# The product-key top-k of an expert layer, with its candidate sums, index arithmetic and lookup made for four heads in one set of instructions

## The chip, the cores and the metric

One core of a Trainium2 chip. The time is device microseconds (us) for one execution of the whole program; lower is better. Of each kernel there is a median of several runs, and one further execution that the hardware profiler recorded.

## What is computed

A decoder trunk of two layers over 256 tokens of width 1024. Each layer has a mixer half (a state-space mixer and two attentions) and an expert half. The expert half is where the change lies. For each token and each of 8 heads it scores two sets of 128 keys, takes the 16 best of either, adds the two lists to candidates, takes the 16 best sums, and looks up which pair of keys each one came from:

```python
q = (xc @ wq).reshape(PEER_CHUNK, PEER_HEADS, 2, PEER_HALF)
s1 = einsum("thd,nd->thn", q[:, :, 0], k1)
s2 = einsum("thd,nd->thn", q[:, :, 1], k2)
v1, i1 = top_k(s1, 16)
v2, i2 = top_k(s2, 16)
cand = (v1[..., :, None] + v2[..., None, :]).reshape(..., 256)
sc, ci = top_k(cand, 16)
e = take_along_axis(i1, ci // 16) * 128 + take_along_axis(i2, ci % 16)
g = softmax(sc)
act = gelu(einsum("td,thkd->thk", xc, u[e])) * g
out = einsum("thk,thkd->td", act, v[e])
```

The kernel gathers nothing: it computes the products with all 16,384 rows of `u` and `v` and weighs them with a matrix of gates built from `e` and `g`.

## The kernel before

Tokens lie on the 128 partitions in two chunks (`NC`), or in the free dimension where channels are on the partitions. Every fp32 product is made of three matmuls (`mm3`, lines 165 to 168): a weight tile is fetched, ScalarE rounds it to a high part (`split`, L159, tile `wH`), VectorE or GpSimd subtracts to get the low part (L162, tile `wL`), and TensorE runs high times high, low times high, high times low. `wH` and `wL` have three buffers each.

The expert half of a layer (`peer`) goes through these steps on TensorE, in the order in which the code is written (a manual schedule for that engine alone; the other engines' queues are ordered by the framework's scheduler):

1. The queries of head 0, then for each head the queries of the next head and the scores of this one (`query`, `scores`). A query is 48 matmuls over two weight tiles. The low part of these tiles is made on GpSimd in two halves of 512 columns.
2. With the last head the first pair of rows of `u` (`u_pair(0)`), then the pairs 1 to 17. A pair is 48 matmuls over two weight tiles of 1024 columns, with the low parts made on GpSimd (`low="gg"`), and a Gelu on ScalarE (L695).
3. Transposes of the found indices `fi` and of the softmax weights `scv` (L794, L795), which ScalarE casts to `idx1`, `idx2`, `wh` (L796 to L798).
4. Pairs 18 and 19, and then the gates, step by step with the other 44 pairs; after them the products with `v`.

On VectorE the top-k runs beside steps 1 and 2. `choose(h, sc)` is called once for each head. `top16` finds 16 maxima and their places with five instructions (`MAX8`, `FIND_INDEX8`, `MATCH_REPLACE8`, `MAX8`, `FIND_INDEX8`), four times per head on 128 scores (tile `sc`) and twice per head on 80 candidates (`cand`). Beside these, each call has 14 other instructions:

- three sums that make the candidates (L742 to L744, 32, 112 and 16 elements per partition),
- a cast of the found places to 16 bits (L750, `fii`, 64 elements),
- seven small steps of index arithmetic on 32 elements (L752 to L761: tiles `r8`, `a0`, `hi`, `fab`; the profile prints a tile's name without digits at its end),
- the lookup: a comparison with a ramp (L764, `eq`, 1024 elements of 16 bits), a product (L765) and a sum (L766, into `fi`).

After the last head come a subtraction of the maximum (L781), the exponential on ScalarE (L783, placed behind the Gelu of pair 15 by `issue_after(gelu[-3])`), and the division (L785 to L788). ScalarE's queue is in order: what stands behind L783 there is the next casts of `wH`.

Of the kernel before, what the change touches and what calls it, by code (L numbers as in the profile page):

```python
# [12 lines left out]
F16 = mybir.dt.float16  # L13
F32 = mybir.dt.float32
F32R = mybir.dt.float32r
U32 = mybir.dt.uint32
AF = mybir.ActivationFunctionType
ALU = mybir.AluOpType
AX = mybir.AxisListType
# [3 lines left out]
P = 128  # L23
D = 1024
S = 256
NC = 2
# [4 lines left out]
PH = 8  # L31
TK = 16
# [5 lines left out]
AHEAD = 3  # L38
GI = 2
NCAND = 80  # L40
RB = 5
RATE = 2.0
PT = (0, 0)
# [39 lines left out]
def trunk(ctx: ExitStack, tc: tile.TileContext, x_in, c_in, ada, cols, rows, w_in, w_out, wq, keysT, uT, vT, fg, out, dbg=None):  # L83
    nc = tc.nc
    V, A, G, T = nc.vector, nc.scalar, nc.gpsimd, nc.tensor
# [25 lines left out]
    iotar = const.tile([P, TK, TK], F16, tag="iotar", name="iotar")  # L111
# [561 lines left out]
    def peer(l, steps):  # L673
# [23 lines left out]
        with tc.tile_pool(name=f"topk{l}", bufs=1, reuse_waits="tile") as tp:  # L697
            def new(shape, tag, dt=F32, bufs=1):
                return tp.tile(shape, dt, tag=tag, name=tag, bufs=bufs)
# [6 lines left out]
            def top16(vals, idx, src):  # L706
                V.max(vals[:, 0:8], src)
                V.max_index(idx[:, 0:8], vals[:, 0:8], src)
                V.match_replace(out=src, in_to_replace=vals[:, 0:8], in_values=src, imm_value=-3.0e38)
                V.max(vals[:, 8:16], src)  # L710
                V.max_index(idx[:, 8:16], vals[:, 8:16], src)
# [3 lines left out]
            def query(h):  # L715
                with pinned() if h == 0 else nullcontext():
                    pq = proj_channels(wq[l], h * D * 256, 256, lambda q: "h")
                q = new([P, 2, S], "q", bufs=2)
                for i in range(2):
                    A.copy(q[:, i, :], pq[i][:, :S])  # L720
                return q
# [7 lines left out]
                A.copy(sc, pscr.rearrange("p (a b) -> p a b", a=4))  # L729
                return sc  # L730

            def choose(h, sc):
                vv = new([P, 2, NC, TK], "vv", bufs=2)
                ii = new([P, 2, NC, TK], "ii", U32, bufs=2)
                for c in range(NC):
                    for i in range(2):
                        top16(vv[:, i, c, :], ii[:, i, c, :], sc[:, 2 * c + i, :])


                cand = new([P, NC, NCAND], "cand", bufs=2)  # L740
                v1, v2 = vv[:, 0], vv[:, 1]
                V.tensor_tensor(out=cand[:, :, 0:16], in0=v1[:, :, 0:1].to_broadcast([P, NC, TK]), in1=v2, op=ALU.add)  # L742
                V.tensor_tensor(out=cand[:, :, 16:72].rearrange("p c (a b) -> p c a b", b=8), in0=v1[:, :, 1:8, None].to_broadcast([P, NC, 7, 8]), in1=v2[:, :, None, 0:8].to_broadcast([P, NC, 7, 8]), op=ALU.add)
                V.tensor_tensor(out=cand[:, :, 72:80], in0=v1[:, :, 8:16], in1=v2[:, :, 0:1].to_broadcast([P, NC, 8]), op=ALU.add)  # L744
                ci = new([P, NC, TK], "ci", U32, bufs=2)
                for c in range(NC):
                    top16(scv[:, c, h, :], ci[:, c, :], cand[:, c, :])

                fii = new([P, 2, NC, TK], "fii", F16, bufs=2)
                V.tensor_copy(fii, ii)  # L750
                r8 = new([P, NC, TK], "r8", U32, bufs=2)
                V.tensor_single_scalar(r8, ci, 3, op=ALU.logical_shift_right)  # L752
                a0 = new([P, NC, TK], "a0", bufs=2)
                V.tensor_scalar(out=a0, in0=r8, scalar1=-1.0, scalar2=0.0, op0=ALU.add, op1=ALU.max)
                hi = new([P, NC, TK], "hi", bufs=2)
                V.tensor_scalar(out=hi, in0=ci, scalar1=-72.0, scalar2=0.0, op0=ALU.add, op1=ALU.max)
                fab = new([P, 2, NC, TK], "fab", F16, bufs=2)
                V.tensor_tensor(out=fab[:, 0], in0=a0, in1=hi, op=ALU.add)
                V.scalar_tensor_tensor(out=a0, in0=a0, scalar=1.0, in1=a0, op0=ALU.min, op1=ALU.add)
                V.scalar_tensor_tensor(out=a0, in0=a0, scalar=-8.0, in1=ci, op0=ALU.mult, op1=ALU.add)  # L760
                V.tensor_tensor(out=fab[:, 1], in0=a0, in1=hi, op=ALU.subtract)  # L761
                eq = new([P, 2 * NC, TK, TK], "eq", F16, bufs=2)
                wide = lambda x: x.rearrange("p i c s -> p (i c) s")
                V.tensor_tensor(out=eq, in0=wide(fab)[:, :, :, None].to_broadcast([P, 2 * NC, TK, TK]), in1=iotar[:, None].to_broadcast([P, 2 * NC, TK, TK]), op=ALU.is_equal)  # L764
                V.tensor_tensor(out=eq, in0=eq, in1=wide(fii)[:, :, None, :].to_broadcast([P, 2 * NC, TK, TK]), op=ALU.mult)  # L765
                V.tensor_reduce(out=wide(fi[:, :, :, h, :]), in_=eq, axis=AX.X, op=ALU.add)  # L766

            q = query(0)
            for h in range(PH):
                q2 = query(h + 1) if h + 1 < PH else None  # L770
                if q2 is None:
                    u_pair(0, act1[:, 0:2, :])
                choose(h, scores(q))
                q = q2
            gelu = [u_pair(ip, act1[:, 2 * ip:2 * ip + 2, :]) for ip in range(1, NA // 2 - LEAD)]


# [262 lines left out]
```

## Time and profile before

| what | us |
|---|---|
| median of 3 runs (lowest, highest) | 1995.51 (1990.01, 1998.99) |
| profiled execution, its own time | 1995.14 |
| its span from first to last instruction | 1993.4 |
| mean granted TensorE clock, of full speed | 0.973 |
| top-k of layer 0, first maximum to last division on VectorE | 198.5 to 353.1 |
| top-k of layer 1, the same | 1184.4 to 1340.2 |

Times of an event count from the span's start. A busy engine is one with an instruction in flight: TensorE's matmuls are pipelined, so that one lasts 284 ns in the list of groups while they start 118 ns apart at full clock and 214 ns apart at half clock. An instruction that waits for a shared resource after it was issued counts as busy, so a wait of that kind shows as a long duration and not as idle time.

### The profile page before, as it was taken

What the parts mean: (1) busy time and instruction counts of PE and PEld (TensorE: products, weight loads), DVE (VectorE), ACT (ScalarE), POOL (GpSimd) and SP (SyncE); (2) the same over time, 40 slices, a digit from 0 to 9 for tenths busy, and PEclk for the clock granted to TensorE, in tenths of its full rate; (3) what the DMA queues carried; (4) which work ended last, traced back from release to release, by engine and by line L of the source; (5) the groups of instructions that cost most, each with busy time, mean ns of one, the idle gap of its engine ahead of it and who ended that gap; (6) DMA issues with size and microseconds to landing.
All of it is one profiled execution on the core that took longest, in us unless ns stands there. A gap on an engine that the chain in (4) does not pass through costs nothing.

```text
span 1993.4 us, 33885 instructions
## 1 busy us (share of the span) xinstructions
PE 1883.4 (94%) x12864; PEld 1717.4 (86%) x12864; DVE 1440.0 (72%) x2746; ACT 966.0 (48%) x1502; POOL 776.0 (39%) x441
## 2 busy tenths in 40 slices
PE   4898998999999998999989989989999999999998
PEld 3787998999999786788877889979999998888886
DVE  6975999889963998855554669998899435555555
ACT  3564544454444444454545544445444444555444
POOL 5775787000024234322246657960000342222333
PEclk9898999999999999999989989989999999999999
DMA  8863554444455998855634334544444555665653
GB/s 285 281 208 124 164 181 165 134 162 155 160 168 177 348 350 311 295 196 193 194 121 138 127 130 149 189 150 155 155 160 159 177 181 190 206 215 192 195 194 116
DMA packets 103559, 376.50 MB, mean 189 GB/s; under 512 B 12002, under 2 KB 12258, under 8 KB 102756
## 3 DMA queue, kind: packets, MB, share of 16 engines
q1 hardware_dynamic: 103396, 374.34, 55.7%
q8 instruction: 100, 1.64, 0.3%
q14 instruction: 63, 0.52, 0.1%
HBM read 371.15 MB, written 3.15 MB: 188 GB/s over the span
## 4 chain that ended last, share of the span: by engine, by line
PE 69%; DVE 21%; POOL 3%; issue 2%; ACT 2%; DMA 2%; SPq 0%; POOLq 0%; ACTq 0%; DVEq 0%
PE pacc L167 11%; PE pacc L168 10%; PE pacc L166 10%; PE pu L166 9%; PE pu L168 9%; PE pu L167 9%; POOL wL L162 2%; PE pa L167 1%; DVE eq L765 1%; PE pa L168 1%; PE pa L166 1%; DVE eq L764 1%; DVE raw L178 1%; DVE fi L766 1%; DVE a L760 1%
## 5 line engine op out<-in xcount | busy, mean ns | idle before, releaser
L162 POOL TENSOR_TENSOR wL<-raw,wH 128x1024 fp32r<-128x1024 f32 (+2 forms) x364 | 719.8, 1992 | 1142.9 <-ACT wH L159 1134.3
L159 ACT CAST wH<-raw 128x1024 fp32r<-128x1024 f32 (+1 forms) x602 | 628.5, 1045 | 517.7 <-PE pu L167 345.2
L166 PE MATMUL pu<-hH,wH 128*128 128x256 f32 x2048 | 581.5, 284 | 4.8 <-ACT wH L159 2.8
L168 PE MATMUL pu<-hH,wL 128*128 128x256 f32 x2048 | 576.2, 281 | 3.8 <-POOL wL L162 3.8
L167 PE MATMUL pu<-hL,wH 128*128 128x256 f32 x2048 | 575.0, 281 | 0.0
L162 DVE TENSOR_TENSOR wL<-raw,wH 128x1024 fp32r<-128x1024 f32 x324 | 399.3, 1233 | 130.9 <-ACT wH L159 130.8
L167 PE MATMUL pacc<-wL,aH 128*128 128x512 f32 x1024 | 401.4, 392 | 11.6 <-POOL wL L162 8.7
L168 PE MATMUL pacc<-wH,aL 128*128 128x512 f32 x1024 | 399.3, 390 | 0.0
L166 PEld LDWEIGHTS pu<-hH,wH 128*128 128x128 f32 x2048 | 387.5, 189 | 5.3 <-ACT wH L159 3.0
L168 PEld LDWEIGHTS pu<-hH,wL 128*128 128x128 f32 x2048 | 388.0, 189 | 4.3 <-POOL wL L162 4.3
L167 PEld LDWEIGHTS pu<-hL,wH 128*128 128x128 f32 x2048 | 388.1, 189 | 0.0
L880 DVE TENSOR_TENSOR aL<-act,aH 128x256 fp32r<-128x256 f32 x256 | 164.1, 642 | 224.2 <-ACT aH L879 223.7
L166 PE MATMUL pacc<-wH,aH 128*128 128x512 f32 x1024 | 277.7, 389 | 1.2 <-ACT wH L159 1.2
L879 ACT CAST aH<-act 128x256 fp32r<-128x256 f32 x256 | 103.9, 407 | 357.0 <-PE pacc L167 354.7
L167 PEld LDWEIGHTS pacc<-wL,aH 128*128 128x128 f32 x1024 | 192.8, 188 | 57.4 <-POOL wL L162 11.7
L166 PEld LDWEIGHTS pacc<-wH,aH 128*128 128x128 f32 x1024 | 191.9, 188 | 41.4 <-ACT wH L159 1.6
L168 PEld LDWEIGHTS pacc<-wH,aL 128*128 128x128 f32 x1024 | 192.8, 188 | 39.6
L166 PE MATMUL pa<-hH,wH 128*128 128x256 f32 x256 | 75.4, 308 | 13.8 <-ACT hH L260 10.9
L167 PE MATMUL pa<-hL,wH 128*128 128x256 f32 x256 | 76.8, 303 | 1.8 <-DVE hL L261 1.8
L168 PE MATMUL pa<-hH,wL 128*128 128x256 f32 x256 | 76.3, 301 | 1.5 <-POOL wL L162 1.5
L178 DVE SCALAR_TENSOR_TENSOR adaw<-adaw,crow 128x1024 f32<-128x1024 f32 x56 | 70.0, 1259 | 1.2 <-ACT crow L130 1.2
L841 DVE SCALAR_TENSOR_TENSOR act<-pc,act 128x160 f32<-128x160 f32 (+30 forms) x126 | 38.4, 305 | 41.2 <-PE pc L835 40.7
(428 smaller groups left out, 2498.6 us busy)
## 6 DMA issues: line engine op xcount, KB each, us to landing
raw<-in_uT_dram SPq DMA_DIRECT2D x256, 512.0 KB, 3.5
raw<-in_vT_dram SPq DMA_DIRECT2D x256, 512.0 KB, 4.2
adaw<-in_ada_dram SPq DMA_DIRECT2D x56, 512.0 KB, 6.1
raw<-in_ada_dram SPq DMA_DIRECT2D x40, 512.0 KB, 4.5
raw<-in_w_in_dram SPq DMA_DIRECT2D x38, 512.0 KB, 4.1
raw<-in_wq_dram SPq DMA_DIRECT2D x32, 512.0 KB, 3.5
raw<-in_w_out_dram SPq DMA_DIRECT2D x16, 512.0 KB, 3.5
raw<-in_w_in_dram SPq DMA_DIRECT2D x8, 392.0 KB, 3.9
```

Of the source, the lines that this page charges most:

```text
L159: A.copy(h[:, :n], src)
L162: eng.tensor_tensor(out=lo[:, o:o + step], in0=src[:, o:o + step], in1=h[:, o:o + step].bitcast(F32), op=ALU.subtract)
L166: T.matmul(o, l[0], r[0], start=start, stop=False)
L167: T.matmul(o, l[0], r[1], start=False, stop=False)
L168: T.matmul(o, l[1], r[0], start=False, stop=stop)
L178: V.scalar_tensor_tensor(out=src, in0=src, scalar=1.0, in1=cond, op0=ALU.mult, op1=ALU.mult, accum_out=modc[:, m, k:k + 1])
L760: V.scalar_tensor_tensor(out=a0, in0=a0, scalar=-8.0, in1=ci, op0=ALU.mult, op1=ALU.add)
L764: V.tensor_tensor(out=eq, in0=wide(fab)[:, :, :, None].to_broadcast([P, 2 * NC, TK, TK]), in1=iotar[:, None].to_broadcast([P, 2 * NC, TK, ...
L765: V.tensor_tensor(out=eq, in0=eq, in1=wide(fii)[:, :, None, :].to_broadcast([P, 2 * NC, TK, TK]), op=ALU.mult)
L841: V.scalar_tensor_tensor(out=a, in0=pv[:, lo:hi, :], scalar=1.0 / WSCALE, in1=a, op0=ALU.mult, op1=ALU.mult)
L879: A.copy(aH, act)
L880: V.tensor_tensor(out=aL, in0=act, in1=aH.bitcast(F32), op=ALU.subtract)
```

## The change

`choose` is called for a group of `GH` = 4 heads instead of one. It first takes the maxima of the four heads, head by head, as their scores come (`next_scores` issues the next head's queries and this head's scores in the same order as before). Then the 14 other instructions are issued once for the whole group, on tiles four times as long, with the candidates' `top16` still once for each head and chunk between them. The tiles of this part have one buffer where they had two.

```diff
+GH = 4
...
-            def choose(h, sc):
-                vv = new([P, 2, NC, TK], "vv", bufs=2)
-                ii = new([P, 2, NC, TK], "ii", U32, bufs=2)
+            def choose(g, scs):
+                hs4 = slice(g * GH, (g + 1) * GH)
+                vv = new([P, 2, NC, GH, TK], "vv")
+                ii = new([P, 2, NC, GH, TK], "ii", U32)
+                for j, sc in enumerate(scs):
+                    sc = sc()
+                    for c in range(NC):
+                        for i in range(2):
+                            top16(vv[:, i, c, j, :], ii[:, i, c, j, :], sc[:, 2 * c + i, :])
+                CG = NC * GH
+                flat = lambda x: x.rearrange("p c h s -> p (c h) s")
+                cand = new([P, CG, NCAND], "cand")
+                v1, v2 = flat(vv[:, 0]), flat(vv[:, 1])
+                V.tensor_tensor(out=cand[:, :, 0:16], in0=v1[:, :, 0:1].to_broadcast([P, CG, TK]), in1=v2, op=ALU.add)
+                V.tensor_tensor(out=cand[:, :, 16:72].rearrange("p c (a b) -> p c a b", b=8), in0=v1[:, :, 1:8, None].to_broadcast([P, CG, 7, 8]), in1=v2[:, :, None, 0:8].to_broadcast([P, CG, 7, 8]), op=ALU.add)
+                V.tensor_tensor(out=cand[:, :, 72:80], in0=v1[:, :, 8:16], in1=v2[:, :, 0:1].to_broadcast([P, CG, 8]), op=ALU.add)
...
-                    top16(scv[:, c, h, :], ci[:, c, :], cand[:, c, :])
+                    for j in range(GH):
+                        top16(scv[:, c, g * GH + j, :], ci[:, c, j, :], cand[:, c * GH + j, :])
...
-                eq = new([P, 2 * NC, TK, TK], "eq", F16, bufs=2)
+                eq = new([P, 2 * CG, TK, TK], "eq", F16)
+                full = [P, 2 * CG, TK, TK]
+                V.tensor_tensor(out=eq, in0=fab.rearrange("p i c s -> p (i c) s")[:, :, :, None].to_broadcast(full), in1=iotar[:, None].to_broadcast(full), op=ALU.is_equal)
+                V.tensor_tensor(out=eq, in0=eq, in1=fii.rearrange("p i c h s -> p (i c h) s")[:, :, None, :].to_broadcast(full), op=ALU.mult)
+                V.tensor_reduce(out=fi[:, :, :, hs4, :].rearrange("p i c h s -> p (i c) (h s)"), in_=eq.rearrange("p (q h) s a -> p q (h s) a", h=GH), axis=AX.X, op=ALU.add)
-            q = query(0)
-            for h in range(PH):
-                q2 = query(h + 1) if h + 1 < PH else None
-                if q2 is None:
-                    u_pair(0, act1[:, 0:2, :])
-                choose(h, scores(q))
-                q = q2
+            qs = [query(0)]
+            def next_scores(h):
+                if h + 1 < PH:
+                    qs.append(query(h + 1))
+                else:
+                    u_pair(0, act1[:, 0:2, :])
+                return scores(qs[h])
+            for g in range(PH // GH):
+                choose(g, [lambda h=h: next_scores(h) for h in range(g * GH, (g + 1) * GH)])
```

The order of instructions on TensorE, ScalarE, GpSimd and SyncE is the same in both programs; only VectorE's differs, and there only within the top-k of the two layers. Three places of layer 0 follow. In the changed program the lines of the sums are L749 to L751, of the cast L759, of the arithmetic L761 to L770, of the lookup L773 to L775, and every line before `choose` is one higher (L707 is L708).

VectorE, behind the maxima of the first scores: before, the rest of head 0 begins right behind its own maxima.

```order
L707 MAX vv<-sc 128x8 x4
L708 MAX_INDEX ii<-vv,sc 128x8 x4
L743 TENSOR_TENSOR cand<-vv 128x2x56
L709 MATCH_REPLACE sc<-vv,sc 128x128 x4
L710 MAX vv<-sc 128x8 x4
L711 MAX_INDEX ii<-vv,sc 128x8 x3
L744 TENSOR_TENSOR cand<-vv 128x2x8
L711 MAX_INDEX ii<-vv,sc 128x8
L742 TENSOR_TENSOR cand<-vv 128x2x16
L750 CAST fii<-ii 128x64
```

Of the change, the same engine where the first sum stands (the maxima of three heads, 60 instructions, lie ahead of these rows):

```order
L708 MAX vv<-sc 128x8 x4
L709 MAX_INDEX ii<-vv,sc 128x8 x4
L750 TENSOR_TENSOR cand<-vv 128x8x56
L710 MATCH_REPLACE sc<-vv,sc 128x128 x4
L711 MAX vv<-sc 128x8 x4
L712 MAX_INDEX ii<-vv,sc 128x8 x3
L751 TENSOR_TENSOR cand<-vv 128x8x8
L712 MAX_INDEX ii<-vv,sc 128x8
L749 TENSOR_TENSOR cand<-vv 128x8x16
L759 CAST fii<-ii 128x256
```

The sums moved from behind the first head to the fourth, and each covers eight rows of 80 candidates instead of two.

VectorE, the first lookup, before (of head 0) and then of the change (of heads 0 to 3):

```order
L764 TENSOR_TENSOR eq<-fab,iotar 128x1024
L708 MAX_INDEX ci<-scv,cand 128x8 x2
L707 MAX vv<-sc 128x8 x4
L765 TENSOR_TENSOR eq<-eq,fii 128x1024
L709 MATCH_REPLACE cand<-scv,cand 128x80 x2
L708 MAX_INDEX ii<-vv,sc 128x8 x4
L743 TENSOR_TENSOR cand<-vv 128x2x56
L766 TENSOR_REDUCE fi<-eq 128x4x16
```

```order
L773 TENSOR_TENSOR eq<-fab,iotar 128x4096
L712 MAX_INDEX ii<-vv,sc 128x8 x4
L708 MAX vv<-sc 128x8 x4
L774 TENSOR_TENSOR eq<-eq,fii 128x4096
L709 MAX_INDEX ii<-vv,sc 128x8 x4
L750 TENSOR_TENSOR cand<-vv 128x8x56
L775 TENSOR_REDUCE fi<-eq 128x4x64
```

The comparison and the product now work on 4096 elements each; maxima of the last heads stand between them.

VectorE, the end of the top-k, before and then of the change:

```order
L761 TENSOR_TENSOR fab<-a_2702,hi 128x32
L758 TENSOR_TENSOR fab<-a_2825,hi 128x32
L764 TENSOR_TENSOR eq<-fab,iotar 128x1024
L759 SCALAR_TENSOR_TENSOR a_2825<-a_2825 128x32
L765 TENSOR_TENSOR eq<-eq,fii 128x1024
L760 SCALAR_TENSOR_TENSOR a_2825<-a_2825,ci 128x32
L766 TENSOR_REDUCE fi<-eq 128x4x16
L761 TENSOR_TENSOR fab<-a_2825,hi 128x32
L764 TENSOR_TENSOR eq<-fab,iotar 128x1024
L765 TENSOR_TENSOR eq<-eq,fii 128x1024
L766 TENSOR_REDUCE fi<-eq 128x4x16
L785 TENSOR_REDUCE zs<-scv 128x16
```

```order
L795 TENSOR_TENSOR scv<-scv,mxs 128x128
L763 TENSOR_SCALAR a_2681<-r_2679 128x128
L767 TENSOR_TENSOR fab<-a_2681,hi 128x128
L768 SCALAR_TENSOR_TENSOR a_2681<-a_2681 128x128
L769 SCALAR_TENSOR_TENSOR a_2681<-a_2681,ci 128x128
L770 TENSOR_TENSOR fab<-a_2681,hi 128x128
L773 TENSOR_TENSOR eq<-fab,iotar 128x4096
L774 TENSOR_TENSOR eq<-eq,fii 128x4096
L775 TENSOR_REDUCE fi<-eq 128x4x64
L799 TENSOR_REDUCE zs<-scv 128x16
```

Before, the last two heads' arithmetic and lookups are woven into each other; now one set of instructions for four heads stands there, with no maxima between the comparison and the product.

## Rows read from the trace of the kernel before

**Rows 1.** The page: busy time of each engine, and the shares of the chain of work that ended last, by engine.

```profile
PE 1883.4 (94%) x12864; PEld 1717.4 (86%) x12864; DVE 1440.0 (72%) x2746; ACT 966.0 (48%) x1502; POOL 776.0 (39%) x441
...
PE 69%; DVE 21%; POOL 3%; issue 2%; ACT 2%; DMA 2%; SPq 0%; POOLq 0%; ACTq 0%; DVEq 0%
```

**Rows 2.** Busy time by stretch, around the top-k of layer 0 and then of layer 1. Columns: from:to, length, busy us and instructions of PE, PEld, DVE, ACT and POOL, granted TensorE clock, DMA share, GB/s.

```profile
240.00:330.00 90.00, 90.00 (x767) 90.00 (x766) 90.00 (x263) 43.30 (x51) 79.33 (x32) 1.00 0.55 182
...
341.00:354.40 13.40, 6.89 (x30) 6.22 (x31) 12.14 (x11) 3.88 (x6) 8.37 (x4) 0.50 0.46 157
...
1229.00:1236.00 7.00, 4.92 (x29) 4.74 (x28) 7.00 (x32) 2.80 (x5) 2.35 (x1) 0.76 0.45 150
...
1331.00:1341.20 10.20, 2.31 (x12) 1.73 (x12) 8.98 (x10) 1.80 (x3) 4.95 (x3) 0.66 0.50 171
```

**Rows 3.** TensorE in order of time, layer 0 and then layer 1: the first transpose of step 3, the first matmul of pair 18, and the first matmul at full clock behind it. Columns: start, duration, engine, line, operation, tiles, shape, count, and the idle time before it with what ended it.

```profile
352.23 0.69 PE L794 MATMUL pc<-ident,fi 128*128 128x128 f32 x2 [5.36 <-DVE fi L766]
...
354.00 0.56 PE L166 MATMUL pu<-hH,wH 128*128 128x256 f32 x1
...
358.16 0.28 PE L167 MATMUL pu<-hL,wH 128*128 128x256 f32 x1
...
1339.16 0.66 PE L794 MATMUL pb<-ident,fi 128*128 128x128 f32 x2 [7.71 <-DVE fi L766]
...
1340.77 0.56 PE L166 MATMUL pu<-hH,wH 128*128 128x256 f32 x1
...
1344.67 0.28 PE L166 MATMUL pu<-hH,wH 128*128 128x256 f32 x1
```

**Rows 4.** ScalarE in order of time, the same columns: the cast that TensorE's end of pair 15 released, and the exponential; layer 0, then layer 1.

```profile
328.10 1.05 ACT L159 CAST wH<-raw 128x1024 fp32r<-128x1024 f32 x1 [1.78 <-PE pu L167]
...
337.98 0.42 ACT L783 ACTIVATE scv<-scv 128x256 f32<-128x256 f32 x1 [7.03 <-DVE scv L781]
...
1317.83 1.05 ACT L159 CAST wH<-raw 128x1024 fp32r<-128x1024 f32 x1 [1.77 <-PE pu L167]
...
1324.77 0.42 ACT L783 ACTIVATE scv<-scv 128x256 f32<-128x256 f32 x1 [4.09 <-DVE scv L781]
```

**Rows 5.** VectorE's groups by line and shape from 197 to 353 us, the 13 of the 14 instructions per head whose durations vary. Columns: line, engine, operation, tiles, shape, count, busy us, mean ns of one, idle us before them.

```profile
L765 DVE TENSOR_TENSOR eq<-eq,fii 128x1024 f16<-128x1024 f16 x8 | 13.3, 1657 | 0.0
L764 DVE TENSOR_TENSOR eq<-fab,iotar 128x1024 f16<-128x1024 f16 x8 | 10.7, 1335 | 0.0
...
L760 DVE SCALAR_TENSOR_TENSOR a<-a,ci 128x32 f32<-128x32 f32 x8 | 9.3, 1168 | 0.0
L742 DVE TENSOR_TENSOR cand<-vv 128x32 f32<-128x32 f32 x8 | 9.2, 1152 | 0.0
...
L750 DVE CAST fii<-ii 128x64 f16<-128x64 uint32 x8 | 8.4, 1046 | 0.0
L744 DVE TENSOR_TENSOR cand<-vv 128x16 f32<-128x16 f32 x8 | 8.3, 1034 | 0.0
L754 DVE TENSOR_SCALAR a<-r 128x32 f32<-128x32 uint32 x8 | 7.9, 992 | 0.0
L743 DVE TENSOR_TENSOR cand<-vv 128x112 f32<-128x112 f32 x8 | 7.4, 924 | 0.0
...
L758 DVE TENSOR_TENSOR fab<-a,hi 128x32 f16<-128x32 f32 x8 | 6.3, 791 | 0.0
L752 DVE TENSOR_SCALAR r<-ci 128x32 uint32<-128x32 uint32 x8 | 6.1, 768 | 0.0
L759 DVE SCALAR_TENSOR_TENSOR a<-a 128x32 f32<-128x32 f32 x8 | 5.1, 632 | 0.0
L761 DVE TENSOR_TENSOR fab<-a,hi 128x32 f16<-128x32 f32 x8 | 4.7, 583 | 0.0
...
L756 DVE TENSOR_SCALAR hi<-ci 128x32 f32<-128x32 uint32 x8 | 2.5, 310 | 0.0
```

**Rows 6.** Single lines over both layers: count, shortest/median/longest duration in ns, first and last start.

```profile
L744 DVE TENSOR_TENSOR cand<-vv x16: 148/1060/1899, 203.1 to 1303.9; 128x16 f32<-128x16 f32 x16
...
L764 DVE TENSOR_TENSOR eq<-fab,iotar x16: 1202/1213/3295, 217.5 to 1333.7; 128x1024 f16<-128x1024 f16 x16
L765 DVE TENSOR_TENSOR eq<-eq,fii x16: 667/686/2872, 219.8 to 1337.1; 128x1024 f16<-128x1024 f16 x16
```

**Rows 7.** In order of time, columns as in rows 3: GpSimd and VectorE where a comparison begins with a low part, GpSimd's usual pace, and VectorE behind the comparison that ended at 296.1.

```profile
278.35 3.48 POOL L162 TENSOR_TENSOR wL<-raw,wH 128x1024 fp32r<-128x1024 f32 x1 [0.42 <-ACT wH L159]
...
278.35 1.21 DVE L764 TENSOR_TENSOR eq<-fab,iotar 128x1024 f16<-128x1024 f16 x1
...
312.27 2.42 POOL L162 TENSOR_TENSOR wL<-raw,wH 128x1024 fp32r<-128x1024 f32 x1 [0.42 <-ACT wH L159]
...
296.06 2.48 DVE L743 TENSOR_TENSOR cand<-vv 128x112 f32<-128x112 f32 x1
```

**Rows 8.** ScalarE in order of time, two casts two tiles apart.

```profile
305.48 1.05 ACT L159 CAST wH<-raw 128x1024 fp32r<-128x1024 f32 x1 [1.78 <-PE pu L167]
...
311.13 1.05 ACT L159 CAST wH<-raw 128x1024 fp32r<-128x1024 f32 x1 [1.78 <-PE pu L167]
```

**Rows 9.** A stall of TensorE in the products with `v` of layer 0 (columns as in rows 3), and the stretch around it (columns as in rows 2).

```profile
692.15 0.50 PE L167 MATMUL pacc<-wL,aH 128*128 128x512 f32 x1 [1.63 <-DVE wL L162]
...
686.00:696.00 10.00, 8.37 (x37) 6.60 (x37) 10.00 (x15) 4.08 (x6) 2.53 (x1) 1.00 0.88 298
```

More of the change, by code (lines that the diff above doesn't have):

```diff
@@ L730, in scores @@
                 return sc
-            def choose(h, sc):
-                vv = new([P, 2, NC, TK], "vv", bufs=2)
-                ii = new([P, 2, NC, TK], "ii", U32, bufs=2)
-                for c in range(NC):
[L736 to L746, printed above, removed]
-                    top16(scv[:, c, h, :], ci[:, c, :], cand[:, c, :])
-                fii = new([P, 2, NC, TK], "fii", F16, bufs=2)
+            def choose(g, scs):
[14 more added lines that the diff above has]
+                V.tensor_tensor(out=cand[:, :, 72:80], in0=v1[:, :, 8:16], in1=v2[:, :, 0:1].to_broadcast([P, CG, 8]), op=ALU.add)
+                ci = new([P, NC, GH, TK], "ci", U32)
+                for c in range(NC):
+                    for j in range(GH):
+                        top16(scv[:, c, g * GH + j, :], ci[:, c, j, :], cand[:, c * GH + j, :])
+                ci = flat(ci)
+                fii = new([P, 2, NC, GH, TK], "fii", F16)
@@ L750, in choose @@
                 V.tensor_copy(fii, ii)
-                r8 = new([P, NC, TK], "r8", U32, bufs=2)
+                r8 = new([P, CG, TK], "r8", U32)
                 V.tensor_single_scalar(r8, ci, 3, op=ALU.logical_shift_right)
-                a0 = new([P, NC, TK], "a0", bufs=2)
+                a0 = new([P, CG, TK], "a0")
                 V.tensor_scalar(out=a0, in0=r8, scalar1=-1.0, scalar2=0.0, op0=ALU.add, op1=ALU.max)
-                hi = new([P, NC, TK], "hi", bufs=2)
+                hi = new([P, CG, TK], "hi")
@@ L756, in choose @@
                 V.tensor_scalar(out=hi, in0=ci, scalar1=-72.0, scalar2=0.0, op0=ALU.add, op1=ALU.max)
-                fab = new([P, 2, NC, TK], "fab", F16, bufs=2)
+                fab = new([P, 2, CG, TK], "fab", F16)
                 V.tensor_tensor(out=fab[:, 0], in0=a0, in1=hi, op=ALU.add)
@@ L761, in choose @@
                 V.tensor_tensor(out=fab[:, 1], in0=a0, in1=hi, op=ALU.subtract)
-                eq = new([P, 2 * NC, TK, TK], "eq", F16, bufs=2)
[L763 to L766, printed above, removed]
-            q = query(0)
-            for h in range(PH):
-                q2 = query(h + 1) if h + 1 < PH else None
-                if q2 is None:
+                eq = new([P, 2 * CG, TK, TK], "eq", F16)
[8 more added lines that the diff above has]
+                else:
                     u_pair(0, act1[:, 0:2, :])
-                choose(h, scores(q))
-                q = q2
+                return scores(qs[h])
+            for g in range(PH // GH):
+                choose(g, [lambda h=h: next_scores(h) for h in range(g * GH, (g + 1) * GH)])
             gelu = [u_pair(ip, act1[:, 2 * ip:2 * ip + 2, :]) for ip in range(1, NA // 2 - LEAD)]
```

## Prediction

> **What bounds the kernel now.** I read the page first. TensorE is busy 94% of the span, but 21% of the chain that ended last lies on VectorE [rows 1], so there are stretches in which TensorE is not what sets the end. The stretches around the top-k show where. From 240 to 330 us TensorE and VectorE are both busy all the time, at full clock, and GpSimd for 79 of 90 us; from 341 to 354.4 TensorE is busy for half the time and has half its clock; layer 1 shows the same from 1331 to 1341.2 [rows 2]. The timeline names what it waits for: the transposes of the found indices stood 5.36 us in layer 0 and 7.71 us in layer 1 until VectorE had made `fi` [rows 3], and before that the exponential stood 7.03 and 4.09 us in ScalarE's queue until VectorE had made its input, with the casts for TensorE's next tiles behind it [rows 4]. So each top-k ends on VectorE.
>
> Next, why VectorE takes 155 us for it. The 13 instructions of a head whose durations vary add up to 99.2 us for the 8 heads [rows 5]. Their shortest durations are far below their means: 148 ns against 1034 for the sum of 16 elements, 1202 for the comparison, 667 against 1657 for the product [rows 5, 6]. With about 0.17 us for each of the eleven small ones, a head needs 11 x 0.17 + 1.20 + 0.67 = 3.7 us undisturbed, 30 us for eight. The other 69 us are waits, 0.67 us per instruction, and no idle time is marked before them. The timeline shows what for: a low part on GpSimd that begins together with a comparison lasts 3.48 us instead of 2.42, and the sum that VectorE issues while GpSimd then works of 112 elements, lasts 2.48 us [rows 7]. The two engines exclude each other for whole instructions.
>
> **Step 1, VectorE's chain.** 14 instructions for each of 8 heads become 14 for each of two groups: 84 fewer per layer, 78 of them of the kinds that wait. The elements stay the same. If one of the 26 that are left waits as long as one did before, the waits are 26 x 0.67 = 17 us, 52 less. If each waits for a whole low part they are 26 x 2.42 = 63 us, 6 less. I take the first, since maxima still stand between most of the 26. The fixed part of the 84 gives some 6 us more (148 ns for 16 elements leaves about 0.13 us fixed, of which neighbours overlap half). Against that VectorE now runs out of work in the first group, since all it may do there is to take maxima as scores come; a head's queries are 48 matmuls at 118 ns, 5.7 us, its maxima about 4.7: at most 8 us of idling. The chain of layer 0 would end near 353 - 52 - 6 + 8 = 303 us, and at worst near 349.
>
> **Step 2, what TensorE gets back.** Without the wait, its end follows from its own pace. Pair 15 ended at 328.0, where it released a cast [rows 4]. Two casts two tiles apart are 5.65 us apart [rows 8], so pairs 16 and 17 end at 339.3, the twelve transposes at 340.7, and pair 18 starts there and not at 354.00 [rows 3]: 13.3 us. From 354.00 to 358.16 it ran at half clock [rows 3]; at 118 ns instead of 214 ns per matmul these 4.16 us would be 2.29, a gain of 1.9. In layer 1 pair 15 ended at 1317.7, so pair 18 could start at 1330.4 and not at 1340.77, 10.4 us, and the half clock until 1344.67 gives 1.7 [rows 3, 4]. One thing takes the place of the wait: the Gelu of pair 17 must free a bank for pair 18, which costs some 0.4 us per layer when TensorE comes without delay. Sum: 13.3 + 1.9 + 10.4 + 1.7 - 0.8 = **26.5 us**. VectorE at 303 us is 36 us ahead of this, so the exact size of step 1 is covered.
>
> **Step 3, what the long instructions cost.** A comparison of 1024 elements holds GpSimd off for 3.48 - 2.42 = 1.06 us [rows 7]; one of 4096 would hold it for 4.3 us, and the product, whose shortest duration is 0.667 us [rows 6], for 4 x 0.54 = 2.15 us. No row shows a hold of that length. GpSimd's reserve: it has 0.42 us idle per tile [rows 7]. The tile that is cast from 311.13 on is multiplied two tiles later, from 316.8 on, and its low part is first used two matmuls on, at 317.0; GpSimd has it ready at 312.27 + 2.42 = 314.7 [rows 7, 8]. So TensorE feels nothing up to 2.3 us. A comparison that gets its turn when a low part ends makes GpSimd 4.3 - 0.42 = 3.9 us late: TensorE stalls 1.6 us. GpSimd then does one low part while the product waits, and the product makes it 2.15 us late again, of which 0.42 are regained: another 1.7. That is 3.3 us for the first group. In the second the arithmetic stands right in front and uses up some of the reserve; I add 0.4. Per layer 7.0, for both **14.0 us**. Bounds: nothing, if GpSimd slips in more often than I think, and 4.7 us per group and a lower clock, as priced below.
>
> The Trainium skill, "SBUF — State Buffer", section "Who interferes with whom", states the rule that speaks against this change: a VectorE instruction with two inputs in SBUF and a GpSimd instruction that reads SBUF take a shared pair of ports in turn, each for its whole length. By it the hold grows with the instruction, as I have it; by sharing instead there would be no 14 us and the time would be the first rival's. The trace agrees for 1024 elements (the 1.06 us above); no row has 4096.
>
> The Trainium skill, "VectorE: DVE Perf Modes", section "The TRN2 errata", prices an instruction at a fixed 58 cycles beside its elements; by that alone 84 fewer are an estimated 5 us per layer and the sum would be some 1985 us. The durations of rows 5 say that here the fixed part is the small one, and the waits the large one.
>
> TensorE's clock is not charged for these stalls: a stall of 1.63 us in the products with `v` left it at 1.00 over the whole stretch [rows 9], while 2.1 us of idling in 1229 to 1236 brought it to 0.76 there [rows 2]. Stalls of 1.6 and 1.7 are nearest to the first.
>
> **Sum.** The profiled execution took 1995.14 us, the median of the runs is 1995.51, so the one can stand for the other. 1995.1 - 26.5 + 14.0 = **1982.6 us**, 0.6% less. A measurement of this kernel tells about 0.5%, 10 us, from no change, so faster means below 1985.5.
>
> **Rivals.**
> - *The long holds cost nothing*: GpSimd gets its turn inside them, or has more reserve. For: no low part that ran late from 240 to 330 us stopped TensorE [rows 2]. Against: the whole comparison held it off [rows 7]. Time 1995.1 - 26.5 = 1968.6.
> - *The clock falls too*: two stalls so near to each other bring TensorE to half clock for some 3.4 us, as in 1229 to 1236 (24% of 7 us lost [rows 2]), 1.7 us for each of four groups. 1982.6 + 6.8 = 1989.4. For: the idling there was only 0.4 us longer than my stalls.
> - *VectorE still ends last*: the fewer instructions wait longer, nearly a whole low part each. Then the chain shortens by 6 + 6 - 8 = 4 us per layer, and TensorE's stalls vanish in its old wait: 1995.1 - 8 = 1987. Against: several small instructions pass between two low parts whenever GpSimd idles for 0.42 us. The fixed price of the Trainium skill, "VectorE: DVE Perf Modes", cited above, belongs to this case.
> - *Slower*: in the second group no maxima stand between arithmetic, comparison and product. If VectorE keeps the ports for all of it, GpSimd is held for 4.3 + 2.15 + about 1 us, less 2.7 of idle time and reserve: a stall of 4.7 us in one piece, and half clock behind it as from 341 to 354.4 [rows 2]; at 10 us of it 5 us more. 9.7 x 4 groups = 39, so 1995.1 - 26.5 + 39 = 2007 us. It decides from 26.5 / 4 = 6.6 us per group on. Against: behind a comparison GpSimd was served before VectorE's next instruction [rows 7].
>
> **How the numbers follow.** Forecast 0.50 (within 4 us of 1982.6, three quarters of it below 1985.5), no cost of the holds 0.15, lower clock 0.17, VectorE still last 0.10, slower 0.08. Faster by over 0.5%: 0.50 x 0.75 + 0.15 + a quarter of the 0.10 with VectorE last, rounded to 0.55; slower by over 0.5%: the slower rival, less the part of it that ends near zero, 0.06; the rest, 0.39, is within. The range goes from the rival without cost, 1968, to above the ones with the lower clock and with VectorE last, 1993.
>
> **What would show it.** Right: `fi` ready by about 305 us of layer 0; no wait of the transposes on VectorE and no 7 us before the exponential; pair 18 near 348 us (340.7 + 7); two low parts per group that last 4 to 7 us, and TensorE's waits on `wL` of 1.5 to 2 us right behind them, at full clock. The 13 lines' waits per instruction stay near 0.7 us. Wrong: transposes that still wait for `fi` (step 1), no waits on `wL` near the two lookups (step 3 down), or a clock at half behind them (step 3 up).

## The result, and the profile after

| kernel | median of its runs, us (lowest, highest) | profiled execution | span | mean clock |
|---|---|---|---|---|
| before | 1996.11 (1990.01, 1998.99), 4 runs | 1995.14 | 1993.4 | 0.973 |
| changed | 1983.48 (1982.84, 1984.44), 4 runs | 1984.44 | 1982.7 | 0.979 |

The ratio of the changed kernel to the one before is 0.9938, with an interval of 0.9925 to 0.9951. That is 0.6% less, 12.6 us between the medians. The forecast was 1982.6.

The page of the changed kernel, busy time and chain, against [rows 1]:

```profile
PE 1880.2 (95%) x12864; PEld 1712.8 (86%) x12864; DVE 1337.3 (67%) x2578; ACT 966.1 (49%) x1502; POOL 787.4 (40%) x441
...
PE 32%; POOL 0%; issue 0%; ACT 0%; DVE 0%; POOLq 0%
```

VectorE lost 103 us of busy time. Its 21% of the chain are gone. The shares add up to a third only, so the chain was not followed through the whole span; I read no more from it than that.

The stretches of [rows 2] again, same columns:

```profile
240.00:330.00 90.00, 84.28 (x710) 83.48 (x710) 70.23 (x184) 39.26 (x45) 81.33 (x30) 1.00 0.52 170
341.00:354.40 13.40, 12.50 (x106) 12.26 (x105) 4.80 (x7) 7.29 (x10) 10.28 (x5) 1.00 0.60 195
1229.00:1236.00 7.00, 7.00 (x56) 7.00 (x55) 7.00 (x20) 2.60 (x3) 3.54 (x1) 0.86 0.12 42
1331.00:1341.20 10.20, 9.68 (x82) 9.68 (x83) 9.34 (x10) 4.85 (x8) 5.07 (x2) 1.00 0.46 154
```

Two opposite things stand here. Where TensorE worked half the time at half clock, it now works nearly all of it at full clock (second and fourth row). From 240 to 330 us, where it had been busy throughout, it now idles for 5.7 us, and VectorE for 20.

TensorE in order of time, as in [rows 3], and ScalarE's exponential, as in [rows 4], layer 0 and then layer 1:

```profile
347.75 0.38 PE L808 MATMUL pc<-ident,fi 128*128 128x128 f32 x2
...
349.47 0.39 PE L167 MATMUL pu<-hH,wH 128*128 128x256 f32 x1 [0.90 <-ACT act L696]
...
1329.80 0.38 PE L808 MATMUL pb<-ident,fi 128*128 128x128 f32 x2
...
1331.52 0.39 PE L167 MATMUL pu<-hH,wH 128*128 128x256 f32 x1 [0.90 <-ACT act L696]
```

```profile
339.42 0.42 ACT L797 ACTIVATE scv<-scv 128x256 f32<-128x256 f32 x1
...
1321.47 0.42 ACT L797 ACTIVATE scv<-scv 128x256 f32<-128x256 f32 x1
```

Neither the transposes nor the exponential wait for VectorE any more (no bracket on their rows). Pair 18 waits 0.90 us in each layer for the Gelu of pair 17.

VectorE's groups from 198 to 342 us, columns as in [rows 5]:

```profile
L773 DVE TENSOR_TENSOR eq<-fab,iotar 128x4096 f16<-128x4096 f16 x2 | 10.7, 5348 | 0.0
...
L708 DVE MAX8 vv<-sc 128x8 f32<-128x128 f32 x32 | 7.2, 275 | 17.5 <-ACT sc L730 17.5
...
L774 DVE TENSOR_TENSOR eq<-eq,fii 128x4096 f16<-128x4096 f16 x2 | 7.0, 3483 | 0.0
L770 DVE TENSOR_TENSOR fab<-a,hi 128x128 f16<-128x128 f32 x2 | 4.0, 1984 | 0.0
...
L768 DVE SCALAR_TENSOR_TENSOR a<-a 128x128 f32<-128x128 f32 x2 | 3.5, 1758 | 0.0
...
L769 DVE SCALAR_TENSOR_TENSOR a<-a,ci 128x128 f32<-128x128 f32 x2 | 0.6, 277 | 0.0
```

Two instructions of a kind instead of eight. The means of the small ones still lie far apart, 277 to 1984 ns where [rows 5] has 310 to 1168: what an instruction takes is mostly what it happens to wait. Over all 26 of the 13 lines, the time above the shortest of each line adds up to 16.9 us in layer 0 and 13.5 in layer 1. That is too little, since a line has only four instructions in this run and the shortest of them can itself have waited: the shortest cast takes 1.38 us here and 0.27 in another kernel with groups of four, the shortest product 2.63 and 2.27. Over the shortest of the same shape in any of these kernels the sums are 21.4 and 18.0 us, 0.82 and 0.69 us per instruction. Before, 104 instructions had 69 and 70, over the shortest of sixteen.

The ports, as in [rows 7]: GpSimd and VectorE at the first comparison of layer 0, then at the second, then GpSimd at the first of layer 1.

```profile
254.69 6.11 POOL L163 TENSOR_TENSOR wL<-raw,wH 128x1024 fp32r<-128x1024 f32 x1 [0.41 <-ACT wH L160]
...
252.29 6.27 DVE L773 TENSOR_TENSOR eq<-fab,iotar 128x4096 f16<-128x4096 f16 x1
...
289.10 2.43 DVE L763 TENSOR_SCALAR a<-r 128x128 f32<-128x128 uint32 x1
...
297.45 6.41 POOL L163 TENSOR_TENSOR wL<-raw,wH 128x1024 fp32r<-128x1024 f32 x1 [0.41 <-ACT wH L160]
...
297.22 4.43 DVE L773 TENSOR_TENSOR eq<-fab,iotar 128x4096 f16<-128x4096 f16 x1
301.68 4.33 DVE L774 TENSOR_TENSOR eq<-eq,fii 128x4096 f16<-128x4096 f16 x1
306.05 4.42 DVE L775 TENSOR_REDUCE fi<-eq 128x256 f32<-128x4096 f16 x1
...
1232.46 4.75 POOL L163 TENSOR_TENSOR wL<-raw,wH 128x1024 fp32r<-128x1024 f32 x1 [5.26 <-ACT wH L160]
```

A low part of 2.42 us takes 6.11 and 6.41 when a comparison of 4096 elements is in its way. The last row of layer 0 ends at 310.5: `fi` is ready 37 us before the transposes.

What that does to TensorE: its waits from 183 to 375 us and then from 1170 to 1360 (engine, tile, line and what it waited for; us in total, times, the longest):

```profile
PE pu L169 <- POOL wL L163: 5.7, 4, 1.7
...
PE pu L167 <- ACT act L696: 0.9, 1, 0.9
...
PE pu L169 <- POOL wL L163: 4.6, 4, 1.7
PE pu L167 <- ACT act L696: 3.0, 2, 2.1
```

Four waits per layer on the low part, one for each long comparison and product; the first ends at 260.85 us, when the late low part does. All are new; the one wait of this kind before, 1.9 us per layer behind the late casts, is gone. The wait of 2.1 us on a Gelu in layer 1 stood before the change too (the idling from 1229 on in [rows 2]).

To separate the top-k from the rest of the program, the span is cut at two places of each layer: TensorE's first matmul of the first scores, and its first matmul of the gates. Between them lies all that the change can touch.

| profiled execution, us | until L0 scores | top-k L0 | between | top-k L1 | rest | span |
|---|---|---|---|---|---|---|
| before | 196.4 | 170.8 | 815.1 | 171.6 | 639.6 | 1993.4 |
| changed | 198.2 | 162.6 | 816.9 | 165.2 | 639.8 | 1982.7 |

The two stretches are 14.6 us shorter. Some 3.8 us came back in the other three parts, which the change doesn't touch; in the kernels below (that with 160 maxima apart) the stretch between varies from 812 to 820 us though its code is the same, so I put that down to the run.

### The profile page after: what moved, and what is told of

It is laid out like the page before. It is cut to its first block, busy times and chain, and to the rows that moved or that the text cites. A ratio compares the mean times of both kernels' runs of the same rounds, so it can differ in the third digit from the quotient of the medians.

```text
span 1982.7 us, 33717 instructions
## 1 busy us (share of the span) xinstructions
PE 1880.2 (95%) x12864; PEld 1712.8 (86%) x12864; DVE 1337.3 (67%) x2578; ACT 966.1 (49%) x1502; POOL 787.4 (40%) x441
## 5 line engine op out<-in xcount | busy, mean ns | idle before, releaser
L163 POOL TENSOR_TENSOR wL<-raw,wH 128x1024 fp32r<-128x1024 f32 (+2 forms) x364 | 729.6, 2019 | 1120.7 <-ACT wH L160 1102.6
L169 PE MATMUL pu<-hH,wL 128*128 128x256 f32 x2048 | 574.0, 280 | 10.3 <-POOL wL L163 10.3
L167 PE MATMUL pa<-hH,wH 128*128 128x256 f32 x256 | 75.0, 306 | 12.5 <-ACT hH L261 9.6
```

Source lines behind the costliest of these rows:

```text
L163: eng.tensor_tensor(out=lo[:, o:o + step], in0=src[:, o:o + step], in1=h[:, o:o + step].bitcast(F32), op=ALU.subtract)
L167: T.matmul(o, l[0], r[0], start=start, stop=False)
L169: T.matmul(o, l[1], r[0], start=False, stop=stop)
```

## The experiments

Theory: TensorE no longer waits for VectorE (worth some 25 us) but waits for GpSimd's low parts, because each long comparison and product keeps GpSimd off for its whole length (worth some 10). Rival: the remaining time is something else, such as VectorE still being too slow, and the waits on `wL` are harmless.

| kernel | median us (of before, same chip) | ratio, interval | top-k L0, L1 | waits on `wL`, L0, L1 |
|---|---|---|---|---|
| changed (4 heads) | 1983.48 (1996.11) | 0.9938 [0.9925, 0.9951] | 162.6, 165.2 | 5.7, 4.6 |
| lookup in four pieces | 1969.21 (1999.01) | 0.9858 [0.9843, 0.9873] | 155.5, 157.2 | none |
| 2 heads | 1972.53 (1999.01) | 0.9869 [0.9854, 0.9884] | 156.7, 160.4 | 0.2, none |
| 8 heads | 1991.98 (1999.01) | 0.9965 [0.9952, 0.9979] | 167.2, 169.1 | 7.8, 6.9 |
| 1 head, new code | 2000.63 (1998.45) | 1.001 [1.0001, 1.002] | 173.0, 171.4 | 2.3, 2.3 |
| 60 maxima more | 1985.83 (1999.01) | 0.9929 [0.9916, 0.9943] | 162.3, 165.8 | 5.7, 3.6 |
| 160 maxima more | 2094.37 (1998.45) | one run | 175.3, 172.0 | 2.6, 1.9 |
| before, low parts in halves | 1972.28 (1998.45) | 0.9872 [0.9855, 0.9888] | 157.5, 160.0 | none |
| before, zeros as low parts | 1975.85 (1998.45) | one run | 155.5, 159.8 | none |
| four pieces and halves | 1974.19 (1998.02) | 0.988 [0.9863, 0.9896] | 157.8, 161.3 | 0.4, 0.5 |

**The long instructions cut in four.** The elements and the grouping stay; a hold is a quarter as long.

```diff
-                V.tensor_tensor(out=eq, in0=..., in1=..., op=ALU.is_equal)
-                V.tensor_tensor(out=eq, in0=eq, in1=..., op=ALU.mult)
+                for b in range(0, 2 * CG, 4):
+                    V.tensor_tensor(out=eq[:, b:b + 4], in0=..., in1=..., op=ALU.is_equal)
+                for b in range(0, 2 * CG, 4):
+                    V.tensor_tensor(out=eq[:, b:b + 4], in0=eq[:, b:b + 4], in1=..., op=ALU.mult)
```

> The changed kernel, with its two long lookup instructions (comparison and product, 4096 elements each) issued in four pieces of 1024; all else of the change stays, and the order on the other four engines too. Theory (ports): the four stalls of TensorE on wL behind the lookups (5.7 us in layer 0 and 2.5 to 3 of the 4.6 us in layer 1, plus the pieces below the wait threshold) vanish, since a piece holds GpSimd only 1.06 us against a reserve of 2.3; VectorE waits some 12 more times per layer at up to 2.4 us each, still 10 us or more ahead of the transposes. Time 1983.5 - 10 = 1973 us (1970 to 1976). Rival (count): what counts is the number of VectorE instructions; 12 more per layer make it no faster, 1984 to 1986 us.

It has the lowest time of all, 0.8 us below the range that I expected: by the ratios the pieces bring some 16 us over the changed kernel where I expected 10. The quicker TensorE of the last section explains some 3 us of that in the profiled execution; the rest is not explained. Of TensorE's waits in the pairs, from 183 to 375 us and then from 1165 to 1360, only those on the Gelus are left; `wL` has no row:

```profile
PE pu L168 <- ACT act L697: 0.9, 1, 0.9
...
PE pu L168 <- ACT act L697: 3.0, 2, 2.1
```

The pieces and the low parts now take turns, two of each here, VectorE and then GpSimd:

```profile
300.97 4.56 DVE L777 TENSOR_TENSOR eq<-fab,iotar 128x1024 f16<-128x1024 f16 x2
...
301.31 6.49 POOL L164 TENSOR_TENSOR wL<-raw,wH 128x1024 fp32r<-128x1024 f32 x2 [0.41 <-ACT wH L161]
```

VectorE pays for it: its waits in layer 0 rise from 21.4 to 44.7 us, over the same shortest durations, and `fi` is ready at 332.8 instead of 310.5. That is covered, so the time falls all the same. That the long holds have a price is shown by this run; its size is better read from the next one, since in layer 1 this execution also had a quicker TensorE.

**Two heads in a group, and eight.** One keeps the holds at 2048 elements, the other makes one of 8192.

```diff
-GH = 4
+GH = 2        (the other kernel: GH = 8)
```

> The changed kernel with groups of two heads instead of four (four sets of the 14 instructions per layer, comparison and product of 2048 elements). Theory (ports): the comparison holds GpSimd 2.15 us and the product 1.1, each under the reserve of 2.3, so TensorE's stalls on wL nearly vanish; VectorE's chain is 28 instructions longer, some 20 us, and ends about 15 us before the transposes are due. 1972 to 1976 us. Rival (count): half of the saved instructions are back, so half of the gain goes: 1988 to 1991 us.

> The changed kernel with one group of eight heads (one set of the 14 instructions per layer, comparison and product of 8192 elements). Theory (ports): the comparison holds GpSimd 8.6 us and the product 4.3: stalls of TensorE of 5.9 and 3.9 us per layer, 9.8 instead of about 6 in layer 0 and 5 in layer 1, and the first is long enough for half clock (3.4 us of it or more, 1.7 us or more lost): 1983.5 + 8 + 4 to 10 = 1995 (1990 to 2002). Rival (count): fewer instructions still, 1979 to 1983 us.

Two heads came as expected. Eight came within the expected time, but with smaller stalls, 7.8 and 6.9 us per layer instead of 9.8, and by the ratios they cost some 5 us more than the changed kernel where I expected 11.5. With two heads the only wait on `wL` is this one, in layer 0:

```profile
PE pu L169 <- POOL wL L163: 0.2, 1, 0.2
```

So a comparison of 2048 fits into GpSimd's reserve here but for 0.2 us, and one of 4096 does not. The difference in the two stretches, 5.9 and 4.8 us, is the price of the long holds: 10.7 us, and the waits that it takes away are 5.7 + 4.6 - 0.2 = 10.1. With eight heads, a low part and the comparison in order of time in layer 0:

```profile
290.09 10.51 POOL L163 TENSOR_TENSOR wL<-raw,wH 128x1024 fp32r<-128x1024 f32 x1 [0.24 <-ACT wH L160]
...
287.62 10.78 DVE L773 TENSOR_TENSOR eq<-fab,iotar 128x8192 f16<-128x8192 f16 x1
```

TensorE's wait for it in the same layer:

```profile
PE pu L169 <- POOL wL L163: 7.8, 2, 5.8
```

And the stretches about the comparison's stall, which ended at 300.65, and behind the product's (columns as in [rows 2]):

```profile
297.00:303.80 6.80, 3.15 (x14) 3.15 (x15) 6.77 (x2) 0.00 (x0) 6.80 (x2) 0.50 0.25 77
307.20:310.60 3.40, 3.40 (x16) 3.40 (x17) 3.40 (x1) 0.00 (x0) 3.40 (x2) 0.50 0.53 169
```

Here the stalls of 5.8 and 2.0 us come with half clock; the changed kernel's four in layer 0, of at most 1.7 us, left it at 1.00 (240 to 330 us). The margin was small: in the changed kernel with 60 maxima more (below) the stall that ended at 1296.15, also of 1.7 us, came with half clock:

```profile
1296.90:1300.30 3.40, 3.40 (x18) 3.40 (x18) 3.40 (x3) 0.00 (x0) 3.40 (x1) 0.50 0.50 154
```

With eight heads VectorE's instructions wait as well. This small step takes 0.26 us undisturbed on 128 elements and 0.16 on 32:

```profile
284.49 2.64 DVE L769 SCALAR_TENSOR_TENSOR a<-a,ci 128x256 f32<-128x256 f32 x1
```

Carried on from the shortest durations with one and with four heads, the 13 instructions wait an estimated 18 us in layer 0. With two heads the 52 wait at least 32 us, and yet that kernel is the faster one: what counts is who is made to wait.

**One head in a group, with the new code.** New tiles, one buffer instead of two, the maxima first, but no grouping.

```diff
-GH = 4
+GH = 1
```

> The changed kernel's code with groups of one head, so that all that is left of the change is one buffer in place of two for the tiles of this part. Theory (ports): 14 instructions per head again, waits as before, so the same time as the kernel before within 5 us. Rival (rewriting or buffers): if the gain came from these and not from the grouping, some of the 13 us stays.

The same as before to 0.1 or 0.2%, and the old waits are back, behind ScalarE's casts:

```profile
PE pu L167 <- ACT wH L160: 12.4, 1, 12.4
PE pu L169 <- POOL wL L163: 2.3, 1, 2.3
```

So the gain is the grouping's, not that of the rewriting around it.

**VectorE made longer.** In the changed kernel, 60 maxima per group that use a small tile (`MAX8` on `hi`), between the arithmetic and the comparison:

```diff
+                emx = new([P, 8], "emx")
+                for _ in range(60):
+                    V.max(emx, hi.rearrange("p c s -> p (c s)"))
```

> The changed kernel with 60 maxima of 128 elements added behind the index arithmetic of each group, which need no port that GpSimd shares: some 12 us more for VectorE per group, 23 us per layer, 46 us in all. Theory (VectorE no longer ends last): its chain had ended 29 us before the division at 340 us of layer 0, so the time stays at 1983.5 within 3 us. Rival (VectorE is still what the top-k ends on): up to 2030 us.

The time is the same as the changed kernel's (ratios 0.9929 and 0.9938, intervals overlap). Only 67 of layer 0's 120 maxima ran before `fi` was done, as the others were issued behind it; `fi` came at 326.2 us instead of 310.5. So the test is weaker than meant, 15.7 us of delay in place of 23. The same with 160 per group:

> The changed kernel with 160 maxima of 128 elements behind the arithmetic of each group, some 31 us of VectorE per group and 62 per layer, which need no shared port. Theory: VectorE's last lookup, at 310 us of layer 0 in the changed kernel, moves to about 370 us, past the 347 us at which the transposes ran; TensorE waits some 24 us per layer for fi, part of the stalls on wL is hidden in that, and half clock follows: about 1984 + 40 to 55 = 2024 to 2039 us. Rival (it is not this chain that the transposes wait for): no more than the 60 maxima cost, 1984 to 1988 us.

This one was missed by far, 2094 for 2039 at most. `fi` of layer 0 came at 359.7 us, 49.2 later, and the transposes waited for it; but the larger part is a wait in the gates, in each layer (layer 0 shown). TensorE's waits from 355 us on:

```profile
PE pc L851 <- ACT act L860: 43.5, 1, 43.5
PE pc L811 <- DVE fi L778: 15.6, 1, 15.6
```

ScalarE's own longest wait from 355 to 450 us shows why. Of layer 0's 320 maxima 153 were issued behind `fi`, among VectorE's first work for the gates, and ScalarE's L860 waits for them:

```profile
ACT act L860 <- DVE emx L773: 42.0, 1, 42.0
```

I had expected all of them ahead of `fi`. The sum closes: the two top-k stretches are 12.7 and 6.8 us longer than the changed kernel's, the two gate stages (first to last matmul of the gates) 252.3 us instead of 206.6, together 111 us where the two profiled times differ by 110. What the run was for can still be read: 49.2 us of delay became 15.6 us of waiting, so VectorE had 33.6 us to spare in layer 0.

**The kernel before, GpSimd's instruction halved.** One word changes (`g`: 1024 columns at once, `h`: twice 512). VectorE's code is that of before, instruction by instruction.

```diff
-        def u_pair(ip, dst, low="gg"):
+        def u_pair(ip, dst, low="hh"):
```

> The kernel before, with one edit: the low parts of the 20 pairs of step 2 and 4 are made on GpSimd in two halves of 512 columns, as those of the queries already are. Nothing is changed on VectorE. Theory (a VectorE instruction waits for the rest of the GpSimd instruction that holds the ports): the instruction to wait for is 1.3 us long instead of 2.4, so the mean wait per instruction falls from 0.67 to about 0.4 us, VectorE's chain from 155 to about 125 us, under the 143 us at which TensorE wants the transposes; the transposes wait no more: 1996 - 20 to 26 = 1970 to 1976 us on a chip where the kernel before takes 1996. Rival (the two engines slow each other by sharing bandwidth, or VectorE's durations are its own): the same elements are read, no gain, 1996 to 2000 us.

As much gain as from two heads in a group, with a smaller effect on VectorE than I expected. Its waits in layer 0 fall from 69 to 53 us, 0.51 us per instruction and not 0.4, and its chain lasts 144 us and not 125. A single wait is shorter, as what it waits for is half as long: 630 and 626 ns on the mean where [rows 5] has 1152 and 1034 for the same two lines. But more instructions have to wait, 63 of the 104 by over 0.1 us where it was 50.

```profile
L742 DVE TENSOR_TENSOR cand<-vv 128x32 f32<-128x32 f32 x8 | 5.0, 630 | 0.0
L744 DVE TENSOR_TENSOR cand<-vv 128x16 f32<-128x16 f32 x8 | 5.0, 626 | 0.0
```

`fi` is ready at 341.5 us, only just in time: the transposes of `fi` wait 0.5 us for it and those of `scv` 1.6 for the division.

**The kernel before, GpSimd writing without reading.** The low parts of the queries and of the first 20 pairs are filled with zeros by GpSimd (`memset`) instead of subtracted; the low part of these weights is left out of the products.

```diff
+        if low == "m":
+            G.memset(lo[:, :n].bitcast(F32), 0.0)
+            return h, lo
...
-        def u_pair(ip, dst, low="gg"):
+        def u_pair(ip, dst, low="mm"):
...
-                    pq = proj_channels(wq[l], h * D * 256, 256, lambda q: "h")
+                    pq = proj_channels(wq[l], h * D * 256, 256, lambda q: "m")
```

> The kernel before, with GpSimd's low parts of the queries and of the 20 pairs replaced by a fill with zeros of the same tile, which reads no SBUF; left out is the low part of these weights, the matmuls stay. Theory (ports): the VectorE instructions with two SBUF inputs (sums, fab, the comparison, the product) lose their waits and fall to their shortest durations, 0.15 to 0.3, 1.2 and 0.67 us; casts and the arithmetic with one input may still wait, on the write side. The chain falls from 155 to under 110 us, the transposes do not wait, about 1970 us where before takes 1996. Rival (durations are VectorE's own): chain and time as before.

All 104 instructions of layer 0 together wait 4.6 us over their shortest, after 69. The means of the comparison and of the smallest sum are within 11 ns of the shortest durations of [rows 6]:

```profile
L767 DVE TENSOR_TENSOR eq<-fab,iotar 128x1024 f16<-128x1024 f16 x8 | 9.7, 1213 | 0.0
...
L747 DVE TENSOR_TENSOR cand<-vv 128x16 f32<-128x16 f32 x8 | 1.2, 152 | 0.0
```

`fi` is ready at 287.7 us with all eight heads done singly. So 64 of the 69 us are waits for GpSimd's subtractions, and the number of instructions by itself costs TensorE nothing here: no transpose waits.

A fill is also shorter than a subtraction, 0.95 us, and GpSimd now works for a third of the time, so fewer waits alone would not tell reading from writing. The rows do, GpSimd and VectorE at two fills:

```profile
248.93 0.95 POOL L162 MEMSET wL<- 128x1024 f32 x1 [2.77 <-PE pu L171]
...
249.46 1.21 DVE L767 TENSOR_TENSOR eq<-fab,iotar 128x1024 f16<-128x1024 f16 x1
...
280.02 0.95 POOL L162 MEMSET wL<- 128x1024 f32 x1 [1.87 <-PE pu L171]
...
280.15 0.85 DVE L757 TENSOR_SCALAR a<-r 128x32 f32<-128x32 uint32 x1
```

The comparison, with two inputs, runs beside the fill at its shortest duration. So do 28 of the 32 two-input instructions that began during a fill in either layer; the other four stand right behind one that waited. The casts and the steps with one tensor input do wait for the fill, as the expectation left open: all 17 that began during one ended 0.03 to 0.06 us after it. In the kernel before, 97 of the 98 instructions of the 13 lines that began while a subtraction ran took over 0.1 us more than their shortest, and one of the 91 that met none.

The fixed price of an instruction by the Trainium skill ("VectorE: DVE Perf Modes", section "The TRN2 errata") explains none of these waits; that an estimate by it would have come to 1985 us is an accident of this case.

**Both remedies.** The changed kernel with the four pieces of the first experiment, and:

```diff
-        def u_pair(ip, dst, low="gg"):
+        def u_pair(ip, dst, low="hh"):
```

> The changed kernel with both remedies at once: the comparison and the product in four pieces each on VectorE, and GpSimd's low parts of the pairs in halves. My theory (either remedy alone already takes all of TensorE's waits on low parts and on VectorE away, so what is left is TensorE's own pace): the same time as the kernel with the four pieces alone, 1967 to 1974 us, no waits on wL of over 0.5 us. Rival (the two engines still cost each other something that only halves on top take away, for example in the start of the top-k): at least 3 us less than the four pieces alone, below 1966.

No gain over the pieces alone, and 0.2 us above the expected range; the intervals of the two ratios overlap. The two top-k stretches are 6.4 us longer than with the pieces alone, of which the quicker TensorE of that execution explains some 3. Once TensorE has hardly a wait of either kind, a still shorter VectorE (`fi` at 313.2 us) buys nothing.

## Why the prediction was right, point by point

- **Step 1, VectorE's chain**: `fi` at 310.5 us, forecast about 305. The waits were the right term: 17 us forecast for 26 instructions, 21.4 and 18.0 measured. Cut by what each instruction adds to the chain, the 13 lines take some 39 us instead of 91, 52 less, and idling for scores adds 5.8 (8 forecast). Three small errors: the waits were 4 us longer in layer 0; of the 6 us of fixed parts some 4 came on top, since neighbours overlap more of them than I thought; and two of the three instructions of the softmax ahead of the exponential (the copy of the maxima and one subtraction), which I had not counted, now wait for the ports, 3.5 us.
- **Step 2, what TensorE gets back**: 26.5 us forecast. With the long holds out of the way (two heads) the two stretches are 14.1 and 11.2 shorter, 25.3. The Gelu of pair 17 costs 0.9 per layer where I had 0.4, a number that no row gave; that makes up 1.0 of the difference of 1.2. One reading was wrong the other way: a layer has six transposes, not twelve, and they take 0.8 us of TensorE and not 1.4, so some 1.4 us stay open. The clock is back at 1.00 in 341 to 354.4 us, as assumed.
- **Step 3, the long holds**: the mechanism is as forecast, and the size of the first group too: the low part was 6.11 - 2.42 = 3.7 us late (3.9 forecast), and TensorE's steps of 1.65 and 1.57 us from matmul to matmul, less the usual 0.12, are stalls of 1.5 and 1.45 for the 1.6 and 1.7. The sum over both layers was too large: 14.0 forecast, 10.7 by the difference to two heads, 10.3 by the waits. About half of it is layer 1's first group. There TensorE's 2.1 us wait on a Gelu comes just before, GpSimd had been idle for 5.26 us when its low part came 1.92 us after the comparison had begun, so it was 4.75 us long and not 6.11, and the stall behind it was 0.4 us instead of 1.6. I had carried layer 0's phase over to layer 1 unread.
- **The sum**: 26.5 - 14.0 = 12.5 forecast; 14.6 in the two stretches, and 12.6 between the medians. The agreement to 0.9 us is partly luck. The too large step 3 and the too large step 2 cancel to 2.1 us, and 3.8 us in the rest of the profiled execution, which the change does not touch, take that back.
- **The rivals**: holds without cost falls by the waits on `wL` and by the runs with two heads and in four pieces. A lower clock, by the 1.00 in 240 to 330 us of layer 0, and in layer 1 from 1236 us on; it comes with eight heads, and once with 60 maxima more behind a stall of the same 1.7 us, so this rival lost narrowly. VectorE still last, by the missing waits of the transposes and by 60 maxima per group that cost nothing clear of noise. The slower one would need GpSimd kept off through comparison and product in one piece; in the second group it got its turn between the two (6.41 us, and TensorE's two stalls are 4.4 us apart). The Trainium skill's rule on the shared ports ("SBUF — State Buffer", section "Who interferes with whom") holds here up to 8192 elements: a low part of 2.42 us became 3.48 behind a comparison of 1024 [rows 7], 6.11 to 6.41 behind 4096, and 10.51 behind 8192.

## What to carry to other kernels

Where VectorE's small instructions last many times their shortest duration with no idle time before them, look at what GpSimd runs at that moment: shortening GpSimd's instruction can be worth as much as rewriting VectorE's code (1972 us by one word here). When instructions are merged, the hold on the other engine grows with the merged length; compare it with that engine's reserve, and cut the long ones into pieces that stay below it. A reserve is read per place: the first comparison and product made TensorE wait 2.7 us in one layer and 1.5 in the other.

## What the runs showed of the hardware that was not expected

In the second group of the changed kernel nearly every second small VectorE instruction lasts 2.43 to 2.46 us and those between them 0.29 (289.10 to 297.2 us). While GpSimd idles for 0.41 us between two low parts, one or two small instructions slip through, and the next stands for a whole low part. So the wait per instruction stays at 0.7 to 0.8 us on the mean though a single one is 2.2 us or nothing.

TensorE's matmuls in the pairs start 118 ns apart nearly everywhere, but for 74 us of layer 1 of the kernel in four pieces they start 113 ns apart, at the same granted clock. The same 28 matmuls there, and with two heads, first and last:

```profile
1239.79 0.28 PE L169 MATMUL pu<-hL,wH 128*128 128x256 f32 x1
...
1242.85 0.28 PE L169 MATMUL pu<-hL,wH 128*128 128x256 f32 x1
```

```profile
1239.76 0.28 PE L168 MATMUL pu<-hL,wH 128*128 128x256 f32 x1
...
1242.94 0.28 PE L168 MATMUL pu<-hL,wH 128*128 128x256 f32 x1
```

3.06 us against 3.18, and some 3 us over the stretch of that execution. The intervals of the two kernels' ratios overlap, so the 1969 us are not to be read as better than the 1972. Shorter stretches of the same step, 2.5 to 11 us, lie in five of the other traces, most of them right behind a wait of TensorE or a stretch at half clock. What sets the step stays open.
